# Transposing q and k in fp32, once per pair of row tiles, and splitting them behind the transpose

## The chip, the cores and the metric

The kernel runs on one core of one Trainium2 chip. Its metric is the time of one execution on the device, in microseconds (us), the median of several runs. Five engines work side by side, each through its own queue in order: TensorE (PE in the profile: matrix products and transposes, with weight loads listed as PEld), VectorE (DVE), ScalarE (ACT), GpSimd (POOL) and SyncE (SP), which issues the transfers from memory. An instruction that needs another engine's result waits at the head of its queue, and all behind it waits too.

## What is computed

Two layers of an encoder over 512 tokens of width 1024, in fp32. Each layer has two attention branches side by side and then an MLP:

```python
proj = h @ w_in[l]
qa, ka, va, qb, kb, vb, gates = jnp.split(proj, IN_SPLITS, axis=-1)
qa = apply_rope(rms_norm(qa.reshape(b, s, HEADS_A, 2, HEAD_DIM), qk_gain_a[l, 0]), cos, sin)
...
sc = jnp.einsum('bhcqd,bhckd->bhcqk', qblk, kt).astype(jnp.float32) * scale
p = jax.nn.softmax(sc, axis=-1)
w = p[:, :, 0] - lam * p[:, :, 1]
return jnp.einsum('bhqk,bhkd->bhqd', w.astype(vt.dtype), vt)
```

Branch A is differential attention (8 heads, each with two pairs of q and k of 64 columns and a v of 128). Branch B is windowed attention in three groups of four heads of 64 columns. Every q and k is normalised per head, multiplied by a gain and rotated before the scores.

## The kernel before

TensorE's products run on a reduced type of the same width (fp32r). To keep precision, an operand is split in two: hi is the rounded copy (made by ScalarE), lo is the difference from it (made by VectorE), and a product is the sum of hi x hi, hi x lo and lo x hi (`mm3`, L275). Weights arrive by a transfer and are split by `split_w` (L259).

**Pieces and slots.** The projection to q, k and v is cut into 14 pieces of 384 columns (`qkv`, L348): two q heads, two k heads and v, 128 columns each. The pieces 0 to 5 belong to branch B, 6 to 13 to the eight heads of branch A. Each piece has four slots, one per row tile of 128 tokens. A slot's work is in parts:

- `part` (L380): 24 products of 128x384 into an accumulator bank, in three runs of 9, 9 and 6;
- `post1` (L393): ScalarE squares q and k and copies v out, VectorE sums the squares and multiplies by gains and rotation into y, GpSimd takes the power and multiplies y by it;
- `post2` (L414): ScalarE rounds y into the tile T (two copies, q once and k twice), VectorE writes the differences into T. T then holds hi and lo of both q heads, each k hi twice, and both k lo;
- `turn` (L425): four fp32r transposes of T into a bank of `tps`, then two ScalarE copies into q2 and k2, of which each column block c has the hi of head c on one half of the partitions and on the other half lo (q2) or hi again (k2);
- `turn_kl` (L434): a fifth transpose, of k lo, into the free quarter of an accumulator bank, and two copies into kl, one by ScalarE and one by VectorE; the other half of kl's partitions is zero.

`scores` (L447) is then two products over 128 partitions: q2 x k2 gives hi x hi + lo x hi, q2 x kl gives hi x lo.

**Order of the work.** In this stretch every engine's queue is written by hand: `order(True)` ties each instruction to the one traced before it on its engine. The loop at L837 makes one pass per slot k (56 in all, then six gate slots and a tail). `post1` of slot k runs in pass k + 1, `post2` at the end of that pass. `turn` of a slot below 18 runs at the start of pass k + 3, of a later one in pass k + 2 behind the second run of products and the scores of side 1; the fifth transpose follows in the third run. (In layer 0 the first piece is computed earlier, and its four slots are turned in passes 7, 9, 11 and 13.)

Attention tiles are placed in the same passes. Branch B: two tiles (side 0 and side 1) in each of the passes 14 to 17 and 26 to 29; a pass later their weights e are transposed in six pieces that take two banks of `tps` (four and two). Branch A: head h has one row tile in each of the passes 30 + 4h to 33 + 4h: scores, row maxima (nm), exponentials (p), the mix of the two maps; two passes later four transposes of p, a copy to wT and the value products; three passes later the copies out (`leave`). In pass 33 + 4h + 4 the head's output is transposed.

A tile's weights are loaded in four parts, one at the start of pass 4p - 3 and three in pass 4p - 1 (L822).

**PSUM.** `tps` has two banks. Accumulators come from `acc` (two banks), in some passes also from the three that the scores use.

Of the kernel before, what the change touches and what calls it, by code (L numbers as in the profile page):

```python
# [10 lines left out]
F32 = mybir.dt.float32  # L11
R32 = mybir.dt.float32r
BF = mybir.dt.bfloat16
I32 = mybir.dt.int32
AF = mybir.ActivationFunctionType
# [6 lines left out]
KT = 8  # L22
# [19 lines left out]
def trunk(ctx, tc, x, c, pos, cols, rows, ada_w, w_qkv, w_gate, w_ba, w_bb, w_out, w_up, w_down, out):  # L42
# [12 lines left out]
    sp = pool("scr", 2)  # L55
# [33 lines left out]
    T_, V_, S_, G_ = Ordered(nc.tensor), Ordered(nc.vector), Ordered(nc.scalar), Ordered(nc.gpsimd)  # L89
    E_ = Ordered(nc.sync)  # L90
    matmul = T_.matmul
    transpose = T_.transpose
# [9 lines left out]
    tps = lambda: tpp.tile([128, 4, 128], F32, name="tp", tag="tp")  # L102
# [19 lines left out]
    identr = consts.tile([128, 128], R32, name="identr")  # L122
# [225 lines left out]
    def qkv(l, p, ab, hT):  # L348

        w, kv, sts = [], [], []  # L350

        def outer(kt):
            if kt == 0:
                begin()
                for t in range(NT):
                    pool_, tag = ((ssp, "s"), (ssp, "s"), (ssp, "s"), (pvp, "pv"))[t]
                    sts[t]["ps"] = pool_.tile([128, 512], F32, name="acc", tag=tag)
            wh, wl = w[kt // 2]
            cw = slice(384 * (kt % 2), 384 * (kt % 2) + 384)
            for t in range(NT):  # L360
                tk = slice(128 * t, 128 * t + 128)
                mm3(sts[t]["ps"][:, :384], hT[kt][0][:, tk], hT[kt][1][:, tk], wh[:, cw], wl[:, cw],
                    kt == 0, kt == KT - 1)

        def load(i, spare=False):
            w.append(split_w(w_qkv[l, p, i], 768, spare=spare))

        def begin():
            kv.extend([big([128, 2, 512], R32, "q2"), big([128, 2, 512], R32, "k2"),
                       big([128, 2, 512], R32, "kl"),  # L370
                       halfp.tile([128, NT, 128], F32, name="v", tag="half")])
            G_.memset(kv[2][64:128, 0].bitcast(F32), 0.0)
            G_.memset(kv[2][0:64, 1].bitcast(F32), 0.0)

        def slot(t):
            st = {}
            sts.append(st)
            tk = slice(128 * t, 128 * t + 128)

            def part(k0, k1, f=None):  # L380
                if k0 == 0:
                    if t == 0:
                        begin()
                    st["ps"] = acc(4 * p + t in WIDE[l])
                for kt in range(k0, k1):
                    wh, wl = w[kt // 2]
                    cw = slice(384 * (kt % 2), 384 * (kt % 2) + 384)
                    mm3(st["ps"][:, :384], hT[kt][0][:, tk], hT[kt][1][:, tk], wh[:, cw], wl[:, cw],
                        kt == 0, kt == KT - 1)
                if k1 == KT and f is not None:  # L390
                    f(st["ps"][:, 384:512])

            def post1():  # L393
                ps, v = st["ps"], kv[3]
                ps4 = ps[:, :256].rearrange("p (a d) -> p a d", d=64)
                sq = sqs[sqn[0] % 2]
                sqn[0] += 1
                S_.activation(sq[:, :, :64], ps4, AF.Square, scale=0.125)
                S_.activation(v[:, t], ps[:, 256:384], AF.Copy)
                ms = small([128, 4], "ms4")  # L400
                rs = small([128, 4], "rs4")
                V_.reduce_sum(ms, sq, axis=AX.X)
                G_.tensor_tensor(rs, ms, half_neg[:, :4], op=OP.pow)
                y = st["y"] = sp.tile([128, 4, 64], F32, name="y", tag="y")
                g = GT[:, t, 2 * ab:2 * ab + 2][:, :, None].to_broadcast([128, 2, 2, 64])
                V_.tensor_mul(y.rearrange("p (a b) d -> p a b d", b=2),
                              ps4.rearrange("p (a b) d -> p a b d", b=2), g)
                sw = sp.tile([128, 4, 2, 8], F32, name="sw")
                V_.tensor_mul(sw, ps4[:, :, :16].rearrange("p a (h d) -> p a h d", h=2)[:, :, ::-1],
                              ST[:, t, ab].rearrange("p a (h d) -> p a h d", h=2))  # L410
                V_.tensor_add(y[:, :, :16], y[:, :, :16], sw.rearrange("p a h d -> p a (h d)"))
                G_.tensor_mul(y, y, rs[:, :, None].to_broadcast([128, 4, 64]))

            def post2():  # L414
                y = st["y"]
                T = sp.tile([128, 12, 64], R32, name="T", tag="T", bufs=3)
                S_.activation(T[:, 0:4:3], y[:, 0:2], AF.Copy)
                S_.activation(T[:, 5:11].rearrange("p (a b) d -> p a b d", a=2)[:, :, 0:2],
                              y[:, 2:4][:, :, None].to_broadcast([128, 2, 2, 64]), AF.Copy)
                V_.tensor_sub(T.rearrange("p (a b) d -> p a b d", a=4)[:, 0:4:3, 1:3],  # L420
                              y.rearrange("p (a b) d -> p a b d", a=2),
                              T.rearrange("p (a b) d -> p a b d", a=2)[:, :, 0:4:3].bitcast(F32))
                st["T"] = T.rearrange("p a d -> p (a d)")

            def turn():  # L425
                q2, k2, kl, _ = kv
                T = st["T"]
                tp = tps()
                for i, a in enumerate((0, 128, 320, 512)):
                    transpose(tp[:, i].bitcast(R32), T[:, a:a + 128], identr)  # L430
                S_.activation(q2[:, :, tk], tp[:, 0:2], AF.Copy)
                S_.activation(k2[:, :, tk], tp[:, 2:4], AF.Copy)

            def turn_kl(o):  # L434
                transpose(o.bitcast(R32), st["T"][:, 640:768], identr)
                S_.activation(kv[2][0:64, 0, tk], o[0:64], AF.Copy)
                V_.tensor_copy(kv[2][64:128, 1, tk], o[64:128])

            return {"bank": lambda: st["ps"],
                    "parts": [lambda f: part(0, 3), lambda f: part(3, 6), lambda f: part(6, 8, f)],  # L440
                    "turn": turn, "kl": turn_kl, "post1": post1, "post2": post2}

        return {"kv": kv, "load": load, "outer": outer, "slots": [slot(t) for t in range(NT)]}

# [160 lines left out]
    LAG = 2  # L605
    STRIDE = 2
    WIDE = ([*range(18, 25)], [*range(13), *range(18, 25)])
    POST = 90
    TURN = 18
    FIRST = 0  # L610
    AHEAD = 4
# [115 lines left out]
    for l in range(DEPTH):  # L727
# [67 lines left out]
        done = 0  # L795
# [29 lines left out]
            loads.setdefault((k - 1, 1), []).append(slots[k]["load"])  # L825
        mods = {k: 16 + i for i, k in enumerate(range(54, 62))}
        MODS = len(mods)
        post1_at, post2_at, turn_at = {}, {}, {}
        for k in range(nq):
            at = k + 1 if k >= done else STRIDE * k + done + FIRST  # L830
            post1_at.setdefault((at, k < done), []).append(slots[k])
            post2_at.setdefault((at + (k < done), k < done), []).append(slots[k])
            if k < TURN:
                turn_at.setdefault((at + 2 + (k < done), False), []).append(slots[k])
            else:
                turn_at.setdefault((at + 1, True), []).append(slots[k])
        for k in range(done, max(len(slots), max(x[0] for x in due) + 1)):  # L837
            def run(*names):
                for side, n in names:
                    for f in due.get((k, side, n), []):  # L840
                        f()
# [7 lines left out]
            parts = slots[k]["parts"] if k < len(slots) else [lambda f: None] * 3  # L849
            for sl in turn_at.get((k, False), []):  # L850
                sl["turn"]()
                sl["kl"]((sl if sl in slots[:done] else slots[k - 1])["bank"]()[:, 384:512])
            for sl in post2_at.get((k, True), []):
                sl["post2"]()
            for sl in post1_at.get((k, False), []):
                sl["post1"]()
            run((0, "leave"), (1, "leave"))
            load(0)
            parts[0](None)
            run((0, "turn"), (0, "score"))  # L860
            load(1)
            run((0, "mix"))
            if k >= POST:
                for sl in post2_at.get((k, False), []):
                    sl["post2"]()
            parts[1](None)
            run((1, "turn"), (1, "score"))
            due_t = turn_at.get((k, True), [])
            for sl in due_t:
                sl["turn"]()  # L870
            load(2)
            parts[2](due_t[0]["kl"] if due_t and k < nq else None)
            if k >= nq:
                for sl in due_t:
                    sl["kl"](tps()[:, 0])
            for sl in post1_at.get((k, True), []):
                sl["post1"]()
            load(3)
            if k < POST:
                for sl in post2_at.get((k, False), []):  # L880
                    sl["post2"]()
            if l == 0 and k in mods:
                ada(0, mods[k])
            run((0, "value"), (1, "value"), (0, "out"), (1, "out"))
# [392 lines left out]
```

## Time and profile before

| | us |
|---|---|
| median of 3 runs | 1866.06 |
| lowest, highest | 1864.5, 1866.31 |
| the profiled execution, its own time | 1865.87 |
| its span, first to last instruction | 1864.1 |
| TensorE busy | 1838.7 (99%) |
| VectorE busy | 1326.1 (71%) |
| ScalarE busy | 1026.2 (55%) |
| GpSimd busy | 315.7 (17%) |

The granted clock of TensorE is 0.998 of full speed over the span. The two attention stretches, in which q and k are turned, lie between 76 and 435 us (layer 0) and between 959 and 1335 us (layer 1). Products overlap in TensorE's pipeline, so its busy share says little; the distance from the start of one instruction to the start of the next tells what each costs. All work is recorded under L81, the helper that keeps the order, so rows are told apart by their tile names: `tp<-identr,T` is a transpose of T into a `tps` bank, `acc<-wh,hT` a product of the projection, `s<-k,q` a score product, `pv<-v,wT` a value product. A row of a timeline gives start, length, engine, line, operation, output and inputs, shape and count.

### The profile page before, as it was taken

How to read it: one execution, taken by the hardware profiler on the slowest of the kernel's cores; microseconds unless marked ns; L12 is line 12 of the kernel's file. 1: busy time of each engine (PE TensorE's matmuls, PEld its weight loads, DVE VectorE, ACT ScalarE, POOL GpSimd, SP SyncE). 2: the span in 40 equal slices, each digit the busy share in tenths (PEclk: the TensorE clock that was granted, in tenths of full speed). 3: DMA queues.
4: the chain of work that ended last, by engine and by line, in shares of the span. 5: the costliest groups of instructions: out<-in, count | busy, mean ns of one | idle time of the engine just before them, and what ended most of it. 6: DMA issues, size and time to landing. Idle time of an engine off the chain costs nothing.

```text
span 1864.1 us, 27212 instructions
## 1 busy us (share of the span) xinstructions
PE 1838.7 (99%) x9976; PEld 1626.5 (87%) x9976; DVE 1326.1 (71%) x2399; ACT 1026.2 (55%) x2315; POOL 315.7 (17%) x407
## 2 busy tenths in 40 slices
PE   7999999999999999999999999999999999999999
PEld 6999999998888888888889999999888888888887
DVE  8765567777575778999876555777545667788786
ACT  5565567776433644445365556777652345445442
POOL 1332224421122000000034232343111100000000
PEclk9999999999999999999999999999999999999999
DMA  8321211114663345544332121112136633333322
GB/s 329 113 69 52 60 44 60 60 58 148 201 227 114 135 128 181 177 158 147 124 118 73 60 69 44 55 48 71 46 121 211 214 109 116 124 113 115 100 76 83
DMA packets 63639, 212.09 MB, mean 114 GB/s; under 512 B 7185, under 2 KB 7569, under 8 KB 63506
## 3 DMA queue, kind: packets, MB, share of 16 engines
q1 hardware_dynamic: 63218, 210.27, 34.4%
q8 instruction: 79, 1.29, 0.3%
q14 instruction: 54, 0.44, 0.1%
q10 hardware_dynamic: 288, 0.09, 0.0%
HBM read 205.09 MB, written 5.24 MB: 113 GB/s over the span
## 4 chain that ended last, share of the span: by engine, by line
PE 86%; DVE 6%; ACT 4%; POOL 2%; issue 1%; DMA 0%; DVEq 0%; POOLq 0%; ACTq 0%; SPq 0%
PE acc L81 73%; PE tp L81 5%; PE s L81 4%; PE pv L81 3%; PE pvb L81 2%; DVE wl L81 1%; POOL rs L81 1%; ACT T L81 1%; DVE e L81 1%; ACT wh L81 1%; ACT e L81 1%; POOL y L81 1%; DVE y L81 1%; DVE ms L81 1%; DVE raw L81 0%
## 5 line engine op out<-in xcount | busy, mean ns | idle before, releaser
L81 PE MATMUL acc<-wh,hT 128*128 128x384 f32 x1792 | 516.3, 346 | 4.5 <-ACT hT L81 3.4
L81 DVE TENSOR_TENSOR wl<-raw,wh 128x1024 fp32r<-128x1024 f32 (+1 forms) x334 | 379.2, 1144 | 164.0 <-ACT wh L81 161.3
L81 ACT ACTIVATE wh<-raw 128x1024 fp32r<-128x1024 f32 (+1 forms) x334 | 326.0, 987 | 303.9 <-PE acc L81 171.7
L81 PE MATMUL acc<-hT,wh 128*128 128x512 f32 (+1 forms) x1632 | 482.4, 378 | 0.0
L81 PEld LDWEIGHTS acc<-hT,wh 128*128 128x128 f32 x1632 | 298.7, 188 | 54.6
L81 PEld LDWEIGHTS acc<-wh,hT 128*128 128x128 f32 x1792 | 329.4, 188 | 10.4 <-ACT hT L81 4.6
L81 PE MATMUL acc<-hT,wl 128*128 128x512 f32 (+1 forms) x816 | 305.9, 378 | 0.5 <-DVE wl L81 0.5
L81 PE MATMUL acc<-wl,hT 128*128 128x384 f32 x896 | 302.2, 337 | 0.8 <-DVE wl L81 0.8
L81 PE MATMUL acc<-wh,uT 128*128 128x512 f32 (+1 forms) x920 | 293.2, 390 | 0.3
L81 PEld LDWEIGHTS acc<-wh,uT 128*128 128x128 f32 x920 | 172.9, 189 | 39.8 <-issue 4.1
L81 POOL TENSOR_TENSOR rs<-ms,half_neg 128x4 f32<-128x4 f32 (+1 forms) x128 | 123.3, 964 | 477.7 <-DVE ms L81 476.5
L81 PEld LDWEIGHTS acc<-hT,wl 128*128 128x128 f32 x816 | 153.5, 188 | 29.3 <-DVE wl L81 1.1
L81 PE MATMUL acc<-wl,uT 128*128 128x512 f32 (+1 forms) x460 | 178.5, 388 | 0.0
L81 PEld LDWEIGHTS acc<-wl,hT 128*128 128x128 f32 x896 | 169.2, 189 | 4.8 <-DVE wl L81 1.9
L81 DVE CUSTOM_DVE_ANT_0 raw<-raw,cbc,colt 128x1024 f32<-128x1024 f32 x96 | 124.2, 1304 | 27.1 <-DMA raw<-in_ada_w 27.0
L81 ACT ACTIVATE p<-s,nm 128x512 f32<-128x512 f32 x128 | 86.9, 684 | 62.0 <-DVE nm L81 62.0
L81 DVE TENSOR_REDUCE nm<-s 128x1 f32<-128x512 f32 x128 | 82.2, 683 | 28.1 <-PE s L81 27.5
L81 PEld LDWEIGHTS acc<-wl,uT 128*128 128x128 f32 x460 | 86.7, 188 | 17.3
L81 DVE TENSOR_TENSOR y<-y,acc 128x512 f32<-128x512 f32 x152 | 99.4, 679 | 0.8 <-PE acc L81 0.5
L81 ACT ACTIVATE wT<-tp 128x512 f32<-128x512 f32 (+1 forms) x128 | 65.9, 542 | 46.1 <-PE tp L81 46.1
L81 ACT ACTIVATE T<-y 128x128 fp32r<-128x128 f32 x224 | 68.6, 357 | 38.9 <-POOL y L81 38.8
L81 DVE TENSOR_TENSOR T<-y,T 128x256 fp32r<-128x256 f32 x112 | 51.4, 459 | 52.9 <-ACT T L81 51.2
(156 smaller groups left out, 2744.4 us busy)
## 6 DMA issues: line engine op xcount, KB each, us to landing
raw<-in_ada_w SPq DMA_DIRECT2D x96, 512.0 KB, 4.3
raw<-in_w_qkv SPq DMA_DIRECT2D x112, 384.0 KB, 3.3
raw<-in_w_up SPq DMA_DIRECT2D x64, 512.0 KB, 4.1
raw<-in_w_down SPq DMA_DIRECT2D x64, 512.0 KB, 3.5
raw<-in_w_gate SPq DMA_DIRECT2D x32, 512.0 KB, 3.6
raw<-in_w_ba SPq DMA_DIRECT2D x16, 512.0 KB, 4.2
raw<-in_w_out SPq DMA_DIRECT2D x16, 512.0 KB, 3.8
xt<-in_x SPq DMA_DIRECT2D x8, 512.0 KB, 6.2
```

Source lines behind the costliest of these rows:

```text
L81: ins = f(*a, **k)
```

## The change

`post2` and `turn_kl` go, and with them the tile T. `turn` does nothing on even row tiles; on odd ones it takes the y tiles of two row tiles, which are now kept in six buffers, and

- makes four fp32 transposes into one `tps` bank: q of both tiles, k of both tiles (before: ten fp32r transposes for two tiles);
- makes six ScalarE copies of 64 partitions x 256 columns, which round to fp32r: q hi of each head, k hi of each head, and k hi of each head once more to the other half of the partitions;
- makes four VectorE differences 64 x 256 from the same bank: q lo of each head, written to the other half of the partitions, and k lo of each head, on its own half.

In passes in which side 1 transposes nothing, the turn of a slot from 18 on moves ahead of side 0's transposes and scores, behind the first run of products. Sums, products, scores and attention are as before.

```diff
-            def post2():
-                y = st["y"]
-                T = sp.tile([128, 12, 64], R32, name="T", tag="T", bufs=3)
...
             def turn():
+                if t % 2 == 0:
+                    return
                 q2, k2, kl, _ = kv
-                T = st["T"]
                 tp = tps()
-                for i, a in enumerate((0, 128, 320, 512)):
-                    transpose(tp[:, i].bitcast(R32), T[:, a:a + 128], identr)
-                S_.activation(q2[:, :, tk], tp[:, 0:2], AF.Copy)
-                S_.activation(k2[:, :, tk], tp[:, 2:4], AF.Copy)
-
-            def turn_kl(o):
-                transpose(o.bitcast(R32), st["T"][:, 640:768], identr)
-                S_.activation(kv[2][0:64, 0, tk], o[0:64], AF.Copy)
-                V_.tensor_copy(kv[2][64:128, 1, tk], o[64:128])
+                for i in range(2):
+                    y = sts[t - 1 + i]["y"].rearrange("p a d -> p (a d)")
+                    for j in range(2):
+                        transpose(tp[:, 2 * j + i], y[:, 128 * j:128 * j + 128], ident)
+                tq, tk_ = (tp[:, 2 * j:2 * j + 2].rearrange("p a b -> p (a b)") for j in range(2))
+                both = slice(128 * t - 128, 128 * t + 128)
+                halves_ = (slice(0, 64), slice(64, 128))
+                for c in range(2):
+                    S_.activation(q2[halves_[c], c, both], tq[halves_[c]], AF.Copy)
+                for c in range(2):
+                    S_.activation(k2[halves_[c], c, both], tk_[halves_[c]], AF.Copy)
+                for c in range(2):
+                    S_.activation(k2[halves_[1 - c], c, both], tk_[halves_[c]], AF.Copy)
+                for lo, hi, src, own in ((q2, q2, tq, False), (kl, k2, tk_, True)):
+                    for c in range(2):
+                        h = halves_[c]
+                        V_.tensor_sub(lo[h if own else halves_[1 - c], c, both], src[h],
+                                      hi[h, c, both].bitcast(F32))
...
             parts[0](None)
+            due_t = turn_at.get((k, True), [])
+            ahead = (k, 1, "turn") not in due
+            if ahead:
+                for sl in due_t:
+                    sl["turn"]()
             run((0, "turn"), (0, "score"))
```

More of the change, by code (lines that the diff above doesn't have):

```diff
@@ L378, in slot, with part @@
             tk = slice(128 * t, 128 * t + 128)
-            def part(k0, k1, f=None):
+            def part(k0, k1):
                 if k0 == 0:
@@ L389, in part @@
                         kt == 0, kt == KT - 1)
-                if k1 == KT and f is not None:
-                    f(st["ps"][:, 384:512])
             def post1():
@@ L403, in post1 @@
                 G_.tensor_tensor(rs, ms, half_neg[:, :4], op=OP.pow)
-                y = st["y"] = sp.tile([128, 4, 64], F32, name="y", tag="y")
+                y = st["y"] = sp.tile([128, 4, 64], F32, name="y", tag="yq", bufs=6)
                 g = GT[:, t, 2 * ab:2 * ab + 2][:, :, None].to_broadcast([128, 2, 2, 64])
@@ L412, in post1 @@
                 G_.tensor_mul(y, y, rs[:, :, None].to_broadcast([128, 4, 64]))
-            def post2():
-                y = st["y"]
-                T = sp.tile([128, 12, 64], R32, name="T", tag="T", bufs=3)
[L417 to L423, printed above, removed]
@@ L439, in slot @@
-            return {"bank": lambda: st["ps"],
-                    "parts": [lambda f: part(0, 3), lambda f: part(3, 6), lambda f: part(6, 8, f)],
-                    "turn": turn, "kl": turn_kl, "post1": post1, "post2": post2}
+                for i in range(2):
[3 more added lines that the diff above has]
+                tq, tk_ = (tp[:, 2 * j:2 * j + 2].rearrange("p a b -> p (a b)") for j in range(2))
@@ L443, in qkv @@
+            return {"parts": [lambda f: part(0, 3), lambda f: part(3, 6), lambda f: part(6, 8)],
+                    "turn": turn, "post1": post1}
         return {"kv": kv, "load": load, "outer": outer, "slots": [slot(t) for t in range(NT)]}
@@ L607, in trunk @@
     WIDE = ([*range(18, 25)], [*range(13), *range(18, 25)])
-    POST = 90
     TURN = 18
@@ L827, in trunk @@
         MODS = len(mods)
-        post1_at, post2_at, turn_at = {}, {}, {}
+        post1_at, turn_at = {}, {}
         for k in range(nq):
@@ L831, in trunk @@
             post1_at.setdefault((at, k < done), []).append(slots[k])
-            post2_at.setdefault((at + (k < done), k < done), []).append(slots[k])
             if k < TURN:
@@ L851, in trunk @@
                 sl["turn"]()
-                sl["kl"]((sl if sl in slots[:done] else slots[k - 1])["bank"]()[:, 384:512])
-            for sl in post2_at.get((k, True), []):
-                sl["post2"]()
             for sl in post1_at.get((k, False), []):
@@ L862, in trunk @@
             run((0, "mix"))
-            if k >= POST:
-                for sl in post2_at.get((k, False), []):
-                    sl["post2"]()
             parts[1](None)
             run((1, "turn"), (1, "score"))
-            due_t = turn_at.get((k, True), [])
-            for sl in due_t:
-                sl["turn"]()
+            if not ahead:
+                for sl in due_t:
+                    sl["turn"]()
             load(2)
[L872 to L875, printed above, removed]
+            parts[2](None)
             for sl in post1_at.get((k, True), []):
@@ L878, in trunk @@
             load(3)
-            if k < POST:
-                for sl in post2_at.get((k, False), []):
-                    sl["post2"]()
             if l == 0 and k in mods:
```

## The prediction

> **What bounds the kernel now.** I read the page first (span, then the chain that ended last), then the busy time by stretches, then TensorE in order of time inside the stage that the change touches, last the groups by shape and the waits.
>
> ```profile
> span 1864.1 us, 27212 instructions
> PE 86%; DVE 6%; ACT 4%; POOL 2%; issue 1%; DMA 0%; DVEq 0%; POOLq 0%; ACTq 0%; SPq 0%
> 1194.00:1222.00 28.00, 28.00 (x184) 26.86 (x183) 21.18 (x50) 20.80 (x66) 10.50 (x14) 1.00 0.19 58
> ```
>
> The third row is 28 us of the differential-attention stage of layer 1: length, then busy time of TensorE, weight load, VectorE, ScalarE and GpSimd, then the granted clock. TensorE is never idle there; VectorE and ScalarE have a quarter of their time free. So TensorE sets the pace of this stage, and what leaves its queue shortens the span, as long as the two other engines' work still comes in time.
>
> One pass of the loop at line 837 in that stage, TensorE alone:
>
> ```profile
> 276.44 0.61 PE L81 MATMUL pv<-v,wT 128*128 128x128 f32 x4
> 276.81 0.42 PE L81 MATMUL acc<-wh,hT 128*128 128x384 f32 x1
> ...
> 278.48 0.60 PE L81 MATMUL tp<-identr,p 128*128 128x128 f32 x4
> 278.84 0.48 PE L81 MATMUL s<-k,q 128*128 128x512 f32 x1
> 279.15 0.39 PE L81 MATMUL s<-kl,q 128*128 128x512 f32 x1
> ...
> 279.85 0.33 PE L81 MATMUL acc<-wh,hT 128*128 128x384 f32 x1
> ...
> 281.42 0.46 PE L81 MATMUL tp<-identr,T 128*128 128x128 f32 x4
> 281.71 0.41 PE L81 MATMUL acc<-wh,hT 128*128 128x384 f32 x1
> 281.96 0.34 PE L81 MATMUL acc<-wl,hT 128*128 128x384 f32 x1
> ...
> 282.83 0.22 PE L81 MATMUL acc<-identr,T 128*128 128x128 f32 x1
> 282.89 1.10 PE L81 MATMUL pv<-v,wT 128*128 128x128 f32 x8
> 283.75 0.42 PE L81 MATMUL acc<-wh,hT 128*128 128x384 f32 x1
> 284.01 0.34 PE L81 MATMUL acc<-wl,hT 128*128 128x384 f32 x1
> ```
>
> Durations overlap, so I cost by the distance from start to start. A pass takes 283.75 - 276.81 = 6.94. Nine 128x384 products take 281.42 - 279.85 = 1.57, 0.174 each; three 128x512 ones 279.85 - 279.15 = 0.70, 0.233 each. The product behind a group of transposes is late by what the group still holds, so that lateness belongs to the group.
>
> **TensorE's part.** The four split transposes (fp32r, from T): 0.29 to the next product, which itself takes 0.25 in place of 0.174: 0.365. The fifth (into the accumulator bank): 0.06 to the eight value products, and a lateness that these inherit. Eight of their distances and the lateness make 284.01 - 282.89 - 0.174 = 0.95; four and the lateness make 1.10 - 0.61 = 0.49 (all eight, less the last four at 276.44); so a distance is 0.115, the lateness 0.03 and the fifth transpose 0.1. Together 0.465 for a row tile. In the passes before slot 18 the five stand together:
>
> ```profile
> 164.54 0.45 PE L81 MATMUL tp<-identr,T 128*128 128x128 f32 x4
> ...
> 164.92 0.41 PE L81 MATMUL acc<-wh,hT 128*128 128x384 f32 x1
> 165.16 0.34 PE L81 MATMUL acc<-wl,hT 128*128 128x384 f32 x1
> ```
>
> 0.62 less 0.174 is 0.45. A layer has 56 row tiles, 18 of this kind and 38 of the other: 2 x (18 x 0.45 + 38 x 0.465) = 51.5.
>
> New are four fp32 transposes for two row tiles. The trace has fp32 transposes of the same shape (tp from p, above): 0.36 to the scores, whose first product then takes 0.31 in place of 0.233: 0.44 for four. 56 pairs make 24.5. **TensorE's work falls by 27 us**; the bounds are narrow, as only operations are used that the trace has. Hidden behind nothing, this is the gain if nothing else becomes late.
>
> **ScalarE and VectorE.** They do not set the end now, but they get other work in another order.
>
> ```profile
> L81 DVE TENSOR_TENSOR T<-y,T 128x256 fp32r<-128x256 f32 x112 | 51.4, 459 | 52.9 <-ACT T L81 51.2 <-ACT v L81 0.6
> 283.34 0.38 ACT L81 ACTIVATE q<-tp 128x256 fp32r<-128x256 f32 x1
> 283.60 0.39 ACT L81 ACTIVATE k<-tp 128x256 fp32r<-128x256 f32 x1
> 283.86 0.27 ACT L81 ACTIVATE kl<-acc 64x128 fp32r<-64x128 f32 x1
> 284.02 0.62 ACT L81 ACTIVATE T<-y 128x128 fp32r<-128x128 f32 x2
> ...
> 284.72 0.29 DVE L81 CAST kl<-acc 64x128 fp32r<-64x128 f32 x1
> 285.04 0.82 DVE L81 TENSOR_TENSOR T<-y,T 128x256 fp32r<-128x256 f32 x1
> ...
> 286.23 0.42 DVE L81 TENSOR_TENSOR y<-acc,GT 128x256 f32<-128x256 f32 x1
> 286.57 0.21 DVE L81 TENSOR_TENSOR sw<-acc,ST 128x64 f32<-128x64 f32 x1
> ```
>
> ScalarE now spends on a row tile the two T copies (0.62) and q, k, kl (283.34 to 284.02, 0.68): 1.3, or 2.6 a pair. The six new copies are 64x256; no row has that shape, the nearest (q, k: 128x256) follow each other every 0.26, so 6 x 0.26 = 1.6: a ScalarE gain of 1.0 a pair. Lower bound is the 64x128 copy's 0.16 (283.86 to 284.02).
>
> VectorE drops 2 x (0.46 + 0.29) = 1.5 a pair and gets four differences 64x256. Bounds for one: 0.29 (the 64x128 copy) and 0.46 (T's difference, 128x256); I take 0.42, the y product, which also has one source in PSUM. Whether consecutive ones overlap matters. sw starts 0.34 behind y, inside its 0.42. But the kl copy, which is on the upper 64 partitions between operations on all 128, is not overlapped: it ends at 285.01 and T starts at 285.04. The four differences change halves every time, so I take 0.455 each, 1.8 in all. [...] With overlap, as sw over y, the four would take 1.45 (0.4 less), and the loss in the attention stage below would be nil: 5 us less in the sum.
>
> The order is what costs:
>
> ```profile
> DVE kl L81 <- ACT kl L81: 52.6, 55, 3.1
> ACT sq L81 <- DVE kl L81: 32.7, 55, 1.6
> ```
>
> The two kl copies write different halves and read different halves of one bank, and yet VectorE's waits for ScalarE's, and the next ScalarE read of that bank (sq) waits for VectorE's. So in this kernel readers of one PSUM bank on two engines take turns. The new differences read the bank that all six copies read: the first starts behind the sixth copy. A turn is then a chain of 0.6 (transposes to their end) + 1.6 + 0.1 + 1.8 = 4.1 us, in which the tp bank (one of two) is held and everything behind the differences on VectorE's queue (post1's sum, gains and rotation; the row maxima; the weight splits) is late. Who waits for that:
>
> *Passes 16 and 18 of each layer* transpose the windowed weights e in six pieces, which needs both tp banks, right behind a turn.
>
> ```profile
> 129.57 0.51 PE L81 MATMUL tp<-identr,T 128*128 128x128 f32 x4
> 130.07 1.56 ACT L81 ACTIVATE wh<-raw 128x768 fp32r<-128x768 f32 x2
> 131.66 0.60 PE L81 MATMUL tp<-identr,e 128*128 128x128 f32 x4
> 132.73 0.44 PE L81 MATMUL tp<-identr,e 128*128 128x128 f32 x2 [0.47 <-ACT k L81]
> ```
>
> Pass 16: TensorE wants the fifth e at 129.57 + 0.44 + 1.57 + 0.44 = 132.0. ScalarE is in two weight copies until 131.6, the six copies end at 133.3, the differences at 135.1. If the bank that comes free is the one of the first e group instead, it is 134.2 (sq, v and a wT copy behind the six). So 2.2 to 3.1, of which 0.6 is already lost now (132.73 against 132.1). Pass 18, where ScalarE is free: wanted 2.45 behind the turn's start, free after 4.1 (the chain) or 3.3 (the first e group's copy behind sq and v): 0.85 to 1.65. Per layer 2.4 to 4.2; I take **6.5 for both**.
>
> *The differential-attention stage.* Turns fall on odd passes, and so do the weight splits for the next piece: three in the passes whose number leaves 3 when divided by four (pass 3, for short), one in pass 1. Durations:
>
> ```profile
> L81 DVE TENSOR_TENSOR wl<-raw,wh 128x768 fp32r<-128x768 f32 x112 | 107.5, 973 | 42.3 <-ACT wh L81 41.7
> L81 ACT ACTIVATE p<-s,nm 128x512 f32<-128x512 f32 x128 | 86.9, 684 | 62.0 <-DVE nm L81 62.0
> L81 DVE TENSOR_REDUCE nm<-s 128x1 f32<-128x512 f32 x128 | 82.2, 683 | 28.1 <-PE s L81 27.5
> 285.04 0.39 ACT L81 ACTIVATE sq<-acc 128x256 f32<-128x256 f32 x1 [0.40 <-DVE kl L81]
> ...
> 286.15 0.84 ACT L81 ACTIVATE wh<-raw 128x768 fp32r<-128x768 f32 x1
> 286.89 0.59 ACT L81 ACTIVATE wT<-tp 128x512 f32<-128x512 f32 x1
> ```
>
> From the start of pass 3: transposes end at 1.57 + 0.6 = 2.2; copies 3.9; differences 5.75; two maxima 7.0; the second exponential 7.8; three weight copies 10.1; the three splits and, between them, the mix (three operations, some 1.2, an estimate by the 0.68 of a maximum) on VectorE 12.5; then pass 0's post1 (a sum, y, sw) has read its accumulator bank at 13.4. TensorE wants that bank two passes on. An even pass is now 6.94 - 0.47 = 6.47, an odd one 6.91: 13.4. Slack nothing. On: pass 0's maxima and second exponential 15.6; pass 1's squares and leave copies (285.04 to 286.15, 1.1), a weight copy (to 286.89, 0.75), six copies (1.6), wT (0.6) 19.7; TensorE's value products of pass 1 want wT 24 products, two groups of transposes and the scores behind its start, 13.4 + 24 x 0.174 + 0.88 + 4 x 0.233 = 19.4. So about 0.3 is lost a head. Pass 2 has neither turn nor split and the lag is gone. 16 heads in two layers: **5 us**, from 0 (the differences overlap: 0.4 less, all slack) to 16 (1 us a head).
>
> **Sum**, against the profiled execution's own time, 1865.87 (span 1864.1): 1865.9 - 27 + 6.5 + 5 = 1850.4. It lies 0.2 below the median of the runs, 1866.06. I say 1850.5. This case's own range is 1844 to 1857. A difference of 0.2% (3.7 us) is about what a measurement of this kernel can tell from none.
>
> **Rivals.**
> 1. *Hidden.* The differences do not wait for all six copies, or ScalarE's spare 1.0 a pair takes up the lag; then only TensorE's 27 counts and the present 0.6 in pass 16 goes too: 1838. For it: a quarter of ScalarE and VectorE is free in the row of 28 us. Against: the kl waits, 55 times.
> 2. *Lag in every head.* A chain longer by 1 us than I count, so that each of 16 heads loses 1.35 in place of 0.3: 1865.9 - 27 + 6.5 + 21.6 = 1867, no change.
> 3. *Slower: VectorE becomes the pace of the attention stage.* If a difference that reads one half and writes the other costs twice the y row (0.85; no row of the trace has such a move), the chain is 1.7 longer a turn. Pass 1 then loses 0.3 + 1.7 = 2.0 a head, 32 us, and the four turns in passes 16 and 18 7 more: 1865.9 - 27 + 13.5 + 32 = 1884. It turns slower than before when a head loses over (27 - 6.5) / 16 = 1.3 us. For it: the chain has no slack. Against: no 64-partition row is slower than its 128-partition neighbour.
> 4. *It does not take work off TensorE*: fp32 transposes cost as much as all it drops. The p row (0.44 for four) excludes it nearly; 1866.
>
> **Chances.** The forecast 0.50, rival 1 0.28, rival 2 0.14 (half of it still a gain), rival 3 0.06, rival 4 0.02. The range 1838 to 1861 leaves out the outer part of rival 2, rivals 3 and 4, and little below rival 1. Faster 0.50 + 0.28 + 0.07 = 0.85; same 0.07; slower 0.08.
>
> **What would show it.** In the changed profile: 224 transposes of y at 0.44 per four, none of T; six copies every 0.26 and then four differences of 0.42, not overlapped, the first behind the sixth copy; pass pairs of the attention stage of 13.4 in place of 13.9, with waits of TensorE for wT once a head of some tenths; waits of 2 to 3 us for a tp bank in passes 16 and 18. I am wrong if differences start between the copies, if TensorE's waits in the attention stage exceed 1 us a head, or if fp32 transposes of y take longer than those of p.

## The result and the profile after

| | us | against before |
|---|---|---|
| before, median of 4 runs | 1866.04 | |
| changed, median of 4 runs (1911.38 to 1915.64) | 1913.13 | 1.0251, 95% interval 1.0239 to 1.0263 |
| predicted | 1850.5 (1838 to 1861) | |

The change makes the kernel 47 us slower; the prediction said 15.5 us faster. The first rows of the changed kernel's page, its span and the shares of the chain that ended last:

```profile
span 1913.5 us, 26469 instructions
PE 82%; ACT 7%; DVE 7%; issue 2%; DMA 1%; POOL 0%; SPq 0%; ACTq 0%; DVEq 0%
```

TensorE's share of the chain fell from 86% to 82%: more of the end is now set by waits. First the parts that were forecast, in the changed kernel's groups by shape (busy us and mean ns of one, then the idle time before them and its releaser):

```profile
L81 ACT ACTIVATE k<-tp 64x256 fp32r<-64x256 f32 x224 | 84.8, 378 | 2.7
L81 DVE TENSOR_TENSOR kl<-tp,k 64x256 fp32r<-64x256 f32 x112 | 47.2, 422 | 1.5
L81 DVE TENSOR_TENSOR q<-tp,q 64x256 fp32r<-64x256 f32 x112 | 47.2, 422 | 133.4 <-ACT k L81 132.7
L81 PE MATMUL tp<-identr,y 128*128 128x128 f32 x224 | 34.1, 273 | 0.7 <-ACT wT L81 0.6
```

All 224 transposes are of y, none of T. A difference takes 422 ns, and the first q difference waits for ScalarE's k copies. This is as predicted. Now the differential-attention stage in order of time. The changed kernel, from the turn in the last pass of a piece (pass 3 of the prediction) to the products of the next piece, all engines:

```profile
306.12 0.60 PE L81 MATMUL tp<-identr,y 128*128 128x128 f32 x4
...
306.76 0.77 ACT L81 ACTIVATE q<-tp 64x256 fp32r<-64x256 f32 x2 [1.15 <-PE tp L81]
...
307.54 1.55 ACT L81 ACTIVATE k<-tp 64x256 fp32r<-64x256 f32 x4
...
309.12 0.86 DVE L81 TENSOR_TENSOR q<-tp,q 64x256 fp32r<-64x256 f32 x2 [2.17 <-ACT k L81]
...
309.99 0.86 DVE L81 TENSOR_TENSOR kl<-tp,k 64x256 fp32r<-64x256 f32 x2
...
310.88 1.29 DVE L81 TENSOR_REDUCE nm<-s 128x1 f32<-128x512 f32 x2
...
311.66 0.69 ACT L81 ACTIVATE p<-s,nm 128x512 f32<-128x512 f32 x1 [1.96 <-DVE nm L81]
...
312.29 0.34 PE L81 MATMUL acc<-wh,hT 128*128 128x384 f32 x1
...
313.00 2.30 ACT L81 ACTIVATE wh<-raw 128x768 fp32r<-128x768 f32 x3
313.87 0.96 DVE L81 TENSOR_TENSOR wl<-raw,wh 128x768 fp32r<-128x768 f32 x1 [1.71 <-ACT wh L81]
...
313.89 0.44 PE L81 MATMUL acc<-wh,hT 128*128 128x384 f32 x1 [1.26 <-ACT wh L81]
...
314.89 0.45 PE L81 MATMUL acc<-wl,hT 128*128 128x384 f32 x1 [0.55 <-DVE wl L81]
```

It reads as one chain. The six copies end at 309.1, and only then do the differences start; they end at 310.85. The row maxima (nm) stand behind them on VectorE, the exponentials (p) wait for the maxima, and the three weight copies (wh) stand behind the exponentials on ScalarE's queue. The first of these weights is wanted by TensorE for the third run of three products of the next piece, and TensorE stands still for it: the wh product starts at 313.89, 1.6 behind the product before it (312.29), so 1.43 late; the wl product starts 1.0 later, 0.82 late. Together 2.25 us a head. The same place before the change, ScalarE's and VectorE's rows and the products that use these weights:

```profile
300.86 1.29 DVE L81 TENSOR_REDUCE nm<-s 128x1 f32<-128x512 f32 x2 [0.95 <-PE s L81]
...
302.92 0.84 ACT L81 ACTIVATE wh<-raw 128x768 fp32r<-128x768 f32 x1
...
303.80 0.96 DVE L81 TENSOR_TENSOR wl<-raw,wh 128x768 fp32r<-128x768 f32 x1 [1.65 <-ACT wh L81]
...
306.35 0.33 PE L81 MATMUL acc<-wl,hT 128*128 128x384 f32 x1
```

There wl is ready at 304.76 and wanted at 306.35: 1.6 us to spare. That slack, and more, is what the change used up. The waits of the whole run of the changed kernel (total us, times, longest):

```profile
PE acc L81 <- ACT wh L81: 25.7, 17, 2.6
...
PE acc L81 <- DVE wl L81: 11.0, 18, 1.4
PE tp L81 <- ACT wT L81: 7.7, 6, 2.4
```

In each layer TensorE waits so eight times: at the first slots of the pieces 8 to 13, and twice behind them, at the weights of the gates (at 438.2 and 458.1 us in layer 0). Where "a head" stands below, it is the 31 us from one such wait at a piece to the next. Behind the wait there is a second loss. TensorE's score products and the first product of the next run, changed kernel:

```profile
315.70 0.54 PE L81 MATMUL s<-k,q 128*128 128x512 f32 x1
316.04 0.63 PE L81 MATMUL s<-kl,q 128*128 128x512 f32 x1
316.47 0.63 PE L81 MATMUL s<-k,q 128*128 128x512 f32 x1
316.90 0.63 PE L81 MATMUL s<-kl,q 128*128 128x512 f32 x1
317.32 0.52 PE L81 MATMUL acc<-wh,hT 128*128 128x384 f32 x1
```

They follow each other every 0.43, where it was 0.233 in the kernel before at a granted clock of 1.00. The granted clock is halved here from about 316.0 to 319.4 (0.50 from 317.4 to 319.0), and over a whole head it is 0.94 (second row below; windows: TensorE, weight load, VectorE, ScalarE, GpSimd busy, then the clock):

```profile
281.00:312.00 31.00, 29.25 (x186) 27.81 (x186) 22.64 (x53) 20.40 (x58) 10.32 (x14) 1.00 0.16 52
312.00:343.00 31.00, 29.19 (x174) 27.57 (x173) 21.15 (x50) 20.51 (x58) 10.50 (x14) 0.94 0.16 52
```

The first row holds such a wait too (1.20 for wh and 0.55 for wl, at 284.5), and yet the clock stays at 1.00; from there to the wait at 313.9 it is 29.4 us, from that one to the next 31.0.

What the wait and the clock cost shows in the length of the stage in layer 0, from the first value product to the last (the two times in each row): before, changed, and the kernel of the seventh experiment below (`both`), in which the wait is gone:

```profile
L81 PE MATMUL pv<-v,wT x256: 270/275/326, 254.7 to 484.3; 128*128 128x128 f32 x128
```

```profile
L81 PE MATMUL pv<-v,wT x256: 270/275/275, 260.5 to 509.1; 128*128 128x128 f32 x128
```

```profile
L81 PE MATMUL pv<-v,wT x256: 270/275/275, 251.4 to 472.5; 128*128 128x128 f32 x128
```

229.6, 248.6 and 221.1 us; in layer 1 it is 228.8, 248.4 and 220.6. So 38.6 of the change in span (1864.1 to 1913.5, 49.4) arise in the two stages, and nearly all the rest ahead of them: the first value product is 5.8 later in layer 0, and from the last one there to the first of layer 1 it is 3.5 more.

### The profile page after: what moved, and what is told of

The parts are those of the page before. It is cut to its first block, busy times and chain, and to the rows that moved or that the text cites. A ratio compares the mean times of both kernels' runs of the same rounds, so it can differ in the third digit from the quotient of the medians.

```text
span 1913.5 us, 26469 instructions
## 1 busy us (share of the span) xinstructions
PE 1842.2 (96%) x9640; PEld 1623.3 (85%) x9640; DVE 1329.9 (70%) x2399; ACT 1011.1 (53%) x2091; POOL 316.4 (17%) x407
## 4 chain that ended last, share of the span: by engine, by line
PE 82%; ACT 7%; DVE 7%; issue 2%; DMA 1%; POOL 0%; SPq 0%; ACTq 0%; DVEq 0%
PE acc L81 70%; PE tp L81 5%; PE s L81 4%; ACT k L81 2%; PE pv L81 2%; DVE wl L81 2%; PE pvb L81 1%; ACT wh L81 1%; ACT q L81 1%; DVE kl L81 1%; ACT p L81 1%; DVE raw L81 1%; DVE q L81 1%; ACT e L81 1%; DVE nm L81 1%
## 5 line engine op out<-in xcount | busy, mean ns | idle before, releaser
L81 PE MATMUL acc<-wh,hT 128*128 128x384 f32 x1792 | 509.1, 347 | 24.0 <-ACT wh L81 17.7
L81 PEld LDWEIGHTS acc<-wh,hT 128*128 128x128 f32 x1792 | 335.6, 193 | 33.3 <-ACT wh L81 21.5
L81 PE MATMUL acc<-wl,hT 128*128 128x384 f32 x896 | 306.9, 343 | 9.1 <-DVE wl L81 9.1
L81 POOL TENSOR_TENSOR rs<-ms,half_neg 128x4 f32<-128x4 f32 (+1 forms) x128 | 127.3, 995 | 516.5 <-DVE ms L81 515.3
L81 ACT ACTIVATE p<-s,nm 128x512 f32<-128x512 f32 x128 | 86.8, 683 | 108.6 <-DVE nm L81 108.6
L81 DVE TENSOR_TENSOR q<-tp,q 64x256 fp32r<-64x256 f32 x112 | 47.2, 422 | 133.4 <-ACT k L81 132.7
L81 PE MATMUL s<-k,q 128*128 128x512 f32 (+1 forms) x224 | 90.8, 412 | 3.2 <-DVE n L81 3.2
```

The source lines that it names most:

```text
L81: ins = f(*a, **k)
```

## The experiments

The theory, called *order* here: the chain of copies, differences, maxima and exponentials makes the next piece's weights late, and nothing else in the change costs much. Rivals: the copies and differences themselves are too much work for ScalarE or VectorE, or it is the tp bank, or where the turn stands in the pass.

**1. Differences behind the maxima** (`defer`). The turn issues its transposes and copies; its four differences are issued behind the two row maxima.

```diff
...
-                for sl in due_t:
-                    sl["turn"]()
+                held = [sl["turn"](True) for sl in due_t]
             run((0, "turn"), (0, "score"))
+            for f in held:
+                if f is not None:
+                    f()
```

> Edit: in passes in which the turn stands ahead of the scores, the four differences are issued behind the two row maxima and not in front of them; the amount of work is the same. Theory (order): in the pass with three weight splits the maxima wait for the four differences, these for the six copies, the exponentials for the maxima, and the next piece's three weight copies stand behind the exponentials on ScalarE's queue, so TensorE idles for weights at the start of the next piece and its clock drops. Then the exponentials come some 2 us earlier, the wait for the first weight copy (1.26 us a head) vanishes, that for a weight difference stays up to 1 us, and the time falls from 1913 to 1872-1890. Rival (amount): ScalarE and VectorE simply have too much to do in that pass, whatever the order: 1905 or more. Rival (tp bank): the bank is held longer here, so TensorE waits for it: slower than 1913.

Measured 1859.35, ratio 0.9958 (0.9944 to 0.9973): 54 us less than the changed kernel, more than expected. Same instructions, another order: so it is not the amount of work. The first split is now done in time but for a few tenths; VectorE's difference, and the wait left in TensorE's weight load:

```profile
304.66 0.96 DVE L81 TENSOR_TENSOR wl<-raw,wh 128x768 fp32r<-128x768 f32 x1 [0.97 <-ACT wh L81]
...
305.67 0.19 PEld L81 LDWEIGHTS acc<-wl,hT 128*128 128x128 f32 x1 [0.34 <-DVE wl L81]
```

**2. The first weight split earlier** (`load1`). The differences stay in front of the maxima; instead one of the three splits is issued ahead of the turn.

```diff
+            load(1)
             due_t = turn_at.get((k, True), [])
...
             run((0, "turn"), (0, "score"))
-            load(1)
```

> Edit: the first of the three weight splits of a pass is issued behind the first run of products, in front of the turn and the scores; the other two stay. Theory (order): TensorE's 1.26 us wait for the first weight copy goes, but the second and third splits still stand behind the exponentials, so a wait of 1 to 2 us for the second weight difference comes in its place: 1885 to 1908. Rival (tp bank or transposes are what is late): no change from 1913.

Measured 1854.07, ratio 0.9928 (0.9913 to 0.9943): 59 us less, again more than expected. The maxima and exponentials are still late (the total of ScalarE's waits for nm is 104.5 us, 108.6 in the changed kernel), and a head takes 27.5 us in place of 31.0. TensorE's products waited 25.7 us for wh and 11.0 for wl in the changed kernel; here no wait for wh is left, and 2.6 for wl. So of what is late there, nearly all the harm comes from the weights.

**3. The old place of the turn** (`late`). In all passes the turn stands behind side 1's scores, as before the change.

```diff
-            ahead = (k, 1, "turn") not in due
+            ahead = False
```

> Edit: no turn stands ahead of the scores; all are behind side 1's place, where they stood before the change. Theory (order): maxima and exponentials are free of the turn, but the second and third weight splits now stand behind its copies and differences, and the lo parts are late for the next pass's scores: the loss moves and gets smaller or stays, 1885 to 1915. Rival (the place ahead is the whole cause): back to 1840-1860.

Measured 1879.58, ratio 1.0068 (1.0053 to 1.0083): 33.5 us less, between the two forecasts, so neither theory's number held. From the waits of this kernel:

```profile
PE tp L81 <- DVE kl L81: 14.7, 14, 1.5
...
PE acc L81 <- DVE wl L81: 6.9, 6, 1.6
```

Most of the wait for weights is gone, since maxima and exponentials now come ahead of the turn. But the transposes of p stand close behind the turn then, and wait for its tp bank until the last k difference is done. Leaving out the move ahead thus takes back 33.5 of the 47 us, and brings another wait: the turn's chain of some 5 us (306.12 to 310.85) has to fit somewhere.

**4. Two copies more** (`eight`). The last two copies of a turn are made twice, so that the chain is longer by a known amount.

```diff
                 for c in range(2):
                     S_.activation(k2[halves_[c], c, both], tk_[halves_[c]], AF.Copy)
-                for c in range(2):
+                for c in (0, 1, 0, 1):
                     S_.activation(k2[halves_[1 - c], c, both], tk_[halves_[c]], AF.Copy)
```

> Edit: the last two of the six copies are made twice (eight copies a turn, the output unchanged). Theory (order): the chain is 0.78 us longer a turn; it counts once a head in the pass with the three splits, with the dropped clock behind it 0.8 to 1.2 us, and in passes 16 and 18: slower than 1913 by 12 to 22 us. Rival (amount or differences alone): ScalarE has a third of its time free over a head, so 1.6 us more a head change less than 5 us.

Measured 1939.53, ratio 1.0393 (1.037 to 1.0416): 26.4 us more than the changed kernel, above the range. Only part of it lies where I looked for it. The wait in a head grew, as it should, from 1.26 to 1.92; but TensorE behind it (layer 1):

```profile
1262.10 0.44 PE L81 MATMUL acc<-wh,hT 128*128 128x384 f32 x1 [1.92 <-ACT wh L81]
...
1263.90 0.48 PE L81 MATMUL s<-k,q 128*128 128x512 f32 x1
1264.22 0.40 PE L81 MATMUL s<-kl,q 128*128 128x512 f32 x1
1264.45 0.40 PE L81 MATMUL s<-k,q 128*128 128x512 f32 x1
```

Here the score products follow every 0.23, at a granted clock of 1.00 (1253 to 1284). A longer wait costs no lower clock in these heads, and they take 30.6 us against 31.0. Most of the difference came from the stretches ahead of the stages: the first value product of layer 0 is at 273.5, 13 us behind the changed kernel's, and between the last one of layer 0 and the first of layer 1 another 6 are lost. There the waits behind a turn grew by about two copies' time: in the passes 16 and 18 of layer 0 from 1.68 and 1.48 to 2.50 and 2.30.

**5. Copies grouped by half** (`grouped`). The three copies of the lower half first, then the three of the upper.

```diff
                 for c in range(2):
                     S_.activation(q2[halves_[c], c, both], tq[halves_[c]], AF.Copy)
-                for c in range(2):
                     S_.activation(k2[halves_[c], c, both], tk_[halves_[c]], AF.Copy)
-                for c in range(2):
                     S_.activation(k2[halves_[1 - c], c, both], tk_[halves_[c]], AF.Copy)
```

> The changed kernel with the six ScalarE copies in another order: all three that read the lower half, then all three that read the upper. Theory (a ScalarE copy is held until the one before it has ended when the half that it reads or writes changes): two of the five steps fall from 0.39 to about 0.26 and three stay, the chain is 0.26 us shorter a turn; where the chain is late in the heads that is worth 0.2 to 0.5 us each: 1900 to 1910. Rival (a copy 64x256 just costs 0.39, whatever stands before it): all five steps stay at 0.39, and the time at 1910 to 1916.

Measured 1902.64, ratio 1.0205 (1.0184 to 1.0226), as expected. ScalarE in one turn of this kernel:

```profile
304.89 0.38 ACT L81 ACTIVATE q<-tp 64x256 fp32r<-64x256 f32 x1 [1.24 <-PE tp L81]
305.17 0.75 ACT L81 ACTIVATE k<-tp 64x256 fp32r<-64x256 f32 x2
305.94 0.38 ACT L81 ACTIVATE q<-tp 64x256 fp32r<-64x256 f32 x1
306.22 0.76 ACT L81 ACTIVATE k<-tp 64x256 fp32r<-64x256 f32 x2
307.01 0.60 ACT L81 ACTIVATE wT<-tp 128x512 f32<-128x512 f32 x1
```

The copy k behind q, with the same halves, starts 0.28 after it, inside its 0.38. All steps at which a half changes are 0.38 to 0.39. Six copies take 2.12 in place of 2.35. But 0.23 at each of the 16 waits is 3.7 of the 10.5 us, and the trace shows what else differs: in layer 1 the first heads have the full clock and a length of 29.2 us, the later ones, like those of layer 0, a clock of 0.94 and 30.8. Two stretches of this kernel:

```profile
1222.00:1253.00 31.00, 29.42 (x185) 27.81 (x184) 21.60 (x52) 20.92 (x61) 11.90 (x16) 1.00 0.17 52
...
1284.00:1315.00 31.00, 29.42 (x175) 27.84 (x174) 21.38 (x51) 20.11 (x57) 10.51 (x14) 0.94 0.18 56
```

The wait in them is the same: 31.00 less 29.42, 1.58 us idle in either row, 1.03 of it for wh. One kernel, one wait, two clocks: the length of the wait alone doesn't decide here whether the clock falls.

**6. TensorE kept busy in the wait** (`fill`). 16 products of 128x128 into a part of the accumulator bank that nothing reads, ahead of the first product that needs the late weights; the output is the same.

```diff
+                    if p > 6 and t == 0 and kt == 2:
+                        for _ in range(16):
+                            matmul(st["ps"][:, 384:512], hT[0][0][:, tk], w[0][0][:, 0:128],
+                                   start=False, stop=False, skip_group_check=True)
```

> The changed kernel with 16 products 128x128 more, into columns of the accumulator bank that nothing reads, ahead of the first product that needs the late weights, in each of the 14 slots of row tile 0 of branch A's pieces (7 or 8 a layer). They give TensorE something to do during the wait and cost some 1 us each where there is no wait. Theory (the clock of TensorE falls because it stands idle in that wait, and the lower clock is a cost of its own of about 1.6 us a head): the granted clock in the attention stage goes back to 1.00 and the time falls to 1885 to 1900. Rival (the clock has another cause, or the waits' second half is enough to lower it): clock 0.94 as now, 1911 to 1925.

Measured 1897.14, ratio 1.0167 (1.0151 to 1.0182): 16 us less, with more work in it, inside the range of the theory. In time order and as a stretch:

```profile
310.13 2.29 PE L81 MATMUL acc<-wh,hT 128*128 128x384 f32 x18
312.74 0.45 PE L81 MATMUL acc<-wl,hT 128*128 128x384 f32 x1 [0.32 <-DVE wl L81]
```

```profile
312.00:343.00 31.00, 30.37 (x197) 28.97 (x197) 22.47 (x53) 21.65 (x62) 10.34 (x14) 1.00 0.16 52
```

The 18 products in the first row are two of the projection and the 16 added. From their start to the wl product it is 2.61, of which two ordinary steps are 0.35: 2.26 lost, the same as the 2.25 of the changed kernel. But the clock stays at 1.00, and a head takes 29.45 instead of 31.0. From the wait at piece 9 to the last piece it is 1.00 over the whole stretch in both layers (283 to 430 and 1198 to 1345 us). At piece 8 the filling doesn't cover the wait (0.88 and 0.55 are left), and in layer 1 the clock falls behind it (0.94 from 1160 to 1191). So in the heads whose wait is filled the clock didn't fall (1.00 in place of 0.94), and the fall had been worth 1.55 us a head (31.0 less 29.45); not every wait without filling brought it.

**7. Both moves together** (`both`). Experiments 1 and 2 in one kernel.

> The changed kernel with two moves at once: the four differences issued behind the two row maxima, and the first of the three weight splits of a head's next piece issued behind the first run of products. Theory (the loss is one wait, for the last weight splits of the next piece): either move alone already took nearly all of it, so the two together add little: 1848 to 1856 (moved splits alone 1854.1, deferred differences alone 1859.4), TensorE's waits for wh and wl under 0.2 us a head. Rival (two waits, one each): the gains add, 54 and 59 us, down to what TensorE's own saving allows: 1838 or less.

Measured 1841.87, ratio 0.9873 (0.9859 to 0.9888): 71 us less than the changed kernel, 12 less than `load1`. It lies below the 1848 to 1856 of the first case and above the rival's 1838. The gains don't add, so it was mostly one wait; but each move alone left a remainder that I had put too low. In the heads TensorE waits no more for wh or wl, and a head takes 27.07 against 28.21 before. These waits in the whole run:

```profile
PE acc L81 <- DVE wl L81: 0.6, 2, 0.3
...
PE acc L81 <- ACT wh L81: 0.3, 1, 0.3
```

**8. Other places for the turns of branch B** (`best`). Both moves; besides, the turns of slots 13 and 15 leave the start of pass k + 3 for the end of pass k + 2, ahead of that pass's value products, and that of slot 17 goes behind the first run of products of pass 19. Every other turn in a pass where side 1 transposes goes to the end of its pass too. In the passes below, the next slot's sums and rotation are issued ahead of the turn. (My expectation calls the first move a pass later. It is the reverse: the turn comes earlier, in slots 13 and 15 by the value products of one pass.)

```diff
-    TURN = 18
+    TURN = 12
...
+            for sl in post1_at.get((k, False), []):
+                sl["post1"]()
             for sl in turn_at.get((k, False), []):
                 sl["turn"]()
-            for sl in post1_at.get((k, False), []):
-                sl["post1"]()
...
-            if not ahead:
-                for sl in due_t:
-                    sl["turn"]()
...
             load(3)
+            if not ahead:
+                for sl in due_t:
+                    sl["turn"]()
```

> Both moves, and besides: from slot 12 on (before: 18) a turn stands one pass later in the order and in passes where side 1 transposes it goes to the end of the pass; in the passes below, the sums and rotations of the next slot are issued ahead of the turn. Theory (what is left beside the attention heads are the waits of 1.8 and 1.6 us for a tp bank in passes 16 and 18 and some of about 1 us in the passes before): these waits shrink by 3 to 5 us a layer, 1838 to 1849. Rival (a turn that is later makes the first scores of its piece late by as much): no better than the two moves alone, 1848 to 1860.

Measured 1833.71, ratio 0.9829 (0.9813 to 0.9846), better than expected. TensorE's value products now run beside the turn's chain, and its wait for wT at the windowed transposes fell, first `both`, then `best`:

```profile
PE tp L81 <- ACT wT L81: 5.9, 4, 1.5
```

```profile
PE tp L81 <- ACT wT L81: 3.0, 5, 0.7
```

The waits of the early passes for sw and v (1.4 and 1.1 us in `both`) are gone. The trace is 8.5 us shorter than that of `both`, all of it ahead of the stages: 5.7 before the first value product of layer 0, 2.7 between the stages. So these passes held it.

**9. The grouped copies on top** (`best2`).

> The version with the moved splits, deferred differences and later turns (1833.7), with the six copies grouped by half as well. The grouping took 10.5 us from the changed kernel, whose heads wait behind ScalarE's queue. Theory (ScalarE's time counts only where TensorE waits behind it, and here it hardly does): within 3 us of 1833.7. Rival (shorter copies shorten every turn): the same 8 to 11 us again, 1823 to 1826.

Measured 1831.89, ratio 0.9813 (0.98 to 0.9826). The interval overlaps that of `best`: the 1.8 us aren't resolved. That is the theory's case; the rival's 8 to 11 us didn't come. The edit that took 10.5 us from the changed kernel takes some 2 here, if anything, where TensorE hardly waits behind ScalarE (in `best` 3.0 us for wT and 0.4 for wh, in the changed kernel 7.7 and 25.7). This version is 34 us faster than the kernel before and 81 faster than the changed one.

## Why the prediction was wrong

**The step that failed** is "Who waits for that" in the differential-attention stage. I followed the chain from pass 3 through copies, differences, maxima, the second exponential and the three weight copies, and then checked only two consumers: the accumulator bank (13.4 against 13.4) and wT (19.7 against 19.4). The weights themselves have a consumer too, and it is the earliest. By the prediction's own numbers the second exponential ends at 7.8, one copy (0.84) and one difference (0.96) make wl ready at 9.6; TensorE wants it in the third run of three products of the next pass, at 6.91 + 0.25 + 6 x 0.174 = 8.2. That is 1.4 late in each head, more than the 1.3 at which I had said the change turns slower. The times were at hand and weren't compared. Measured: 2.25. I had named the condition under which I would be wrong, "if TensorE's waits in the attention stage exceed 1 us a head", and it is what came; but I had not looked for it in the right queue. Experiments 1 and 2 show the cause from two sides: moving the differences alone takes back 54 us and moving the split alone 59, of the 71 that both together take back.

**A term mis-sized**: ScalarE's six copies, "every 0.26". They are 0.39 apart, 2.35 a turn in place of 1.6. I had asked whether VectorE's differences overlap when halves change, and not asked it of ScalarE. With 0.75 more, the 1.4 above becomes 2.15, which is the 2.25 measured within 0.1.

**A cost not reckoned**: the lower clock behind the wait, 1.55 a head (experiment 6). Together 2.25 + 1.55 = 3.8 us a head, and 31.0 less the 27.07 of `both` is 3.9. Fourteen of the 16 waits lie in the stages, two of them (at 284.5 and 1383.3) without the lower clock; 14 x 3.8 less 2 x 1.55 is 50 us, an estimate that takes the waits at the gates for those at the pieces. From the first value product to the last the changed kernel is behind `both` by 27.5 in layer 0 and 27.8 in layer 1, 55 us where I had put 5. Another 19 lie ahead of the stages (9.1 before the first value product of layer 0, 9.7 between the stages). The wait at piece 8 stands there, where it is longest (2.6 for wh), again with half the clock behind it (0.51 from 256 to 258). Not in the sum either: TensorE's waits for sw and v in the first passes of layer 0, 2.6 us against 0.6 before.

**What was right.** TensorE's work: I said 0.98 less a head (four row tiles at 0.465 less two times 0.44); from before to `both` it is 1.14. For 28 pieces in two layers 1.14 would make 32, an estimate from one head's length; so the 27 us are in the change, and `best` is 32 below the kernel before. The differences: 0.42 each, four in 309.12 to 310.88, 0.44 apart and not overlapped, the first behind the sixth copy. Rival 3's price for a difference that crosses halves, 0.85, is refuted; its sign came true by another mechanism. Passes 16 and 18: predicted 6.5 for both layers; in the changed kernel TensorE waits 1.68 and 1.48 there in layer 0, 2.44 and 1.48 in layer 1, 7.1 in all, of which 1.0 stood before.

**Rival 1** (hidden, 1838) was nearly right about what the edit is worth once the order fits: `both` is 1841.9. Its mechanism didn't hold: the differences do wait for all six copies, and the changed kernel's order didn't take up the lag. A number that comes out of another order is luck.

## What to carry to other kernels

When work is put into an in-order queue, list every instruction behind it and its consumer, and compare each with when it is wanted, most of all loads and splits that seem to belong to the next piece: the first deadline decides, not the last. A change that takes work off the bound engine can need another order of the other engines to be worth anything: the same edit was 47 us slower in one order and 34 us faster in another. And where a unit is never idle now, a first wait can cost more than its own length: here, in most heads, 3.8 us for 2.25.

## What was not expected of the hardware

- ScalarE copies of 64 partitions whose halves differ from the last copy's are not overlapped: they take 0.38 and start 0.39 apart, against 0.28 when input and output stay on their halves (experiment 5).
- TensorE's clock fell to half (0.50) for about 3.4 us behind waits of 1.26 and 0.55 us that make it 2.25 us late, and not behind 1.92 and 0.55 in `eight`, nor behind 1.20 and 0.55 at 284.5 in the changed kernel; in `grouped` the same 1.58 us of idle time came with the fall and without it. What makes one wait bring it and an equal one not, these runs don't show.
